# GpSimd's elementwise work in the norms and in the MLP is given to VectorE and ScalarE

## The chip, the core and the metric

The kernel runs on one core of one Trainium2 chip. A core has a matrix engine (TensorE), two elementwise engines (VectorE and ScalarE), a third, programmable one (GpSimd, POOL in the profile) and SyncE, which here issues the DMAs. Each engine works through its own list of instructions in order; semaphores connect the lists. The metric is the device time of one execution in microseconds, the median of several runs.

## The reference, cut to what matters

Two layers work on a sequence of 1024 frames of width 1024, in float32. Each layer is

```python
mixed = hybrid_mixer(rmsnorm(h, norm_pre_mix[l]), ...)   # mLSTM, GLA and retention heads
h = h + rmsnorm(mixed, norm_post_mix[l])
ff = square(relu(rmsnorm(h, norm_pre_ffn[l]) @ w_ff1[l])) @ w_ff2[l]     # d_ff = 4096
h = h + rmsnorm(ff, norm_post_ffn[l])
# rmsnorm(x, g) = x * rsqrt(mean(x * x, axis=-1) + 1e-6) * g
```

The four rmsnorms of a layer and the square between the two MLP products are what the change is about. The mixer's GLA part, with its chunks of scores built in seven levels, stays as it is.

## The kernel before, in words

Activations are kept transposed: a tile holds 128 features (partitions) by 512 frames, and eight such tiles are one half of the sequence. Each layer is done half by half.

Every large product has float32 accuracy out of three passes: both operands are split into a high part (rounded to float32r) and a low part (the rest), and `mm3` (lines 267 to 270) issues low x high, high x low, high x high. `wslot` (253) loads a 512-row block of weights, casts it on ScalarE (263) and subtracts on VectorE (264); three such blocks may be alive. `split` (272) does the same with an activation: cast on ScalarE (276), subtraction (277). `fm_group` (280) computes two 128x512 output tiles in the two PSUM buffers tagged `d`; a buffer can be refilled only after its evacuation `evac` has read it.

The MLP of one half (`ffn_steps`, 861) runs in eight chunks of 512 hidden features. `f1` is the first product: each of its 128x512 results is read out of PSUM by a Relu on ScalarE (873), squared into the high part on ScalarE (876), squared once more at full precision on GpSimd (877), and the low part is the difference on VectorE (878). `f2` is the second product, whose results are added to an accumulator on VectorE (897). `f1` of a chunk is issued two chunks ahead of the `f2` that reads it. There are 4 x 32 results of `f1`.

A norm has a sum of squares over the eight tiles, a matmul with a matrix of ones that adds over the partitions and hands the sum to every partition (`rstd_begin`, 331), a reciprocal square root on ScalarE and VectorE (`rstd_end`, 336), and the scaling:

- `out_proj` (838) evacuates each of its eight tiles on ScalarE (846), squares it on ScalarE (857) and adds it to `sso` (858), with a lower priority; the add is on GpSimd, but for the last, which is on VectorE.
- `post_norm_end` (383) has two VectorE instructions for each tile, 390 and 391, the second of which adds the residual.
- `square_sum` (345) squares the resulting eight tiles on ScalarE (350, 353) and adds seven of them (354): four on GpSimd, the last three on VectorE. The squares share three buffers of the tag `nt` with the tiles of `pre_norm_end`.
- `pre_norm_end` (362) scales each tile on VectorE (366) and splits it: cast on ScalarE, subtraction on VectorE, but for tiles 2 and 5 on GpSimd.

`mix_norms` (1012) chains a post-norm, the sum and a pre-norm after a mixer, `ffn_norms` (1030) the same after an MLP. These and the mixers are generators: the main list of products calls `tick` after each output tile, and the generator goes on by a step, so that small matmuls are put between large ones. TensorE's order is thereby written out; where a generator's matmul waits, all later products wait behind it.

On the other engines the order is set by a planner when the program is built: it takes the instructions that are ready by its own account of costs, highest priority first. Evacuations have 9000, weight blocks 6000, the norms 2500, the sums of `out_proj` 1500. On the chip the order is fixed, and an instruction at the head of an engine's list that has to wait holds up all behind it.

The main program begins at line 1126. Norms run beside products in four places: `mix_norms(0, 0)` at about 385 to 435 us, `ffn_norms(0, 0)` and `mix_norms(0, 1)` at about 850 to 1000 us, the same pair one half later (1450 to 1600 us), and `mix_norms(1, 1)` at about 2035 to 2095 us.

Of the kernel before, what the change touches and what calls it, by code (L numbers as in the profile page):

```python
# [10 lines left out]
F32 = mybir.dt.float32  # L11
# [3 lines left out]
AF = mybir.ActivationFunctionType  # L15
ALU = mybir.AluOpType
# [3 lines left out]
P = 128  # L20
# [3 lines left out]
KT = D // P  # L24
NH = 2
TH = T // NH
# [20 lines left out]
def hybrid_trunk(ctx, tc, a, out):  # L47
    nc = tc.nc
    V, S, G = nc.vector, nc.scalar, nc.gpsimd
# [23 lines left out]
    tp = ctx.enter_context(tc.tile_pool(name="tp", bufs=4))  # L73
# [67 lines left out]
    def pcol(l, key, i):  # L141
        if key == "mixn":
            c = 64 + 4 * l + i if i < 4 else 72 + 2 * l + i - 4 if i < 6 else 76 + 2 * l + i - 6
        elif key == "conv":
            c = 80 + 16 * l + i
        elif key == "gbias":
            c = 112 + l
        else:
            c = {"pre_mix": 0, "post_mix": 16, "pre_ffn": 32, "post_ffn": 48}[key] + 8 * l + i
        return prm[:, c:c + 1]  # L150
# [121 lines left out]
    def split(src, name, eng=V):  # L272

        hi = up.tile([P, TH], F32R, tag="uh", name=f"uh_{name}")
        lo = up.tile([P, TH], F32R, tag="ul", name=f"ul_{name}")
        S.copy(out=hi, in_=src)  # L276
        eng.tensor_tensor(out=lo, in0=src, in1=hi.bitcast(F32), op=ALU.subtract)  # L277
        return hi, lo

    def fm_group(w, u, evac, name):  # L280

        nk = w.shape[0] // 512
        sl = [wslot(w[512 * k:512 * (k + 1), :], 256, f"{name}_{k}") for k in range(nk)]
        ps = [pd.tile([P, 512], F32, tag="d", name=f"d_{name}_{m}") for m in range(2)]
        for k in range(nk):
            for m in range(2):
                for j in range(4):
                    uh, ul = u[4 * k + j]
                    mm3(ps[m], sl[k][0][:, j, m * P:(m + 1) * P], sl[k][1][:, j, m * P:(m + 1) * P],
                        uh, ul, k == 0 and j == 0, k == nk - 1 and j == 3)  # L290
                if k == nk - 1:
                    with tc.high_priority(offset=EPRIO):
                        rest = evac(m, ps[m])
                    if rest:
                        with tc.high_priority(offset=RPRIO):
                            rest()
                tick()
# [47 lines left out]
    def square_sum(tiles, name):  # L345
        ss = None
        for kt in range(KT):
            if kt == 0:
                ss = np_.tile([P, TH], F32, tag="ss", name=f"ss_{name}", bufs=3)
                S.activation(out=ss, in_=tiles[0], func=AF.Square)  # L350
            else:
                sq = np_.tile([P, TH], F32, tag="nt", name=f"sq_{name}_{kt}", bufs=3)
                S.activation(out=sq, in_=tiles[kt], func=AF.Square)
                (V if kt >= KT - 3 else G).tensor_tensor(out=ss, in0=ss, in1=sq, op=ALU.add)
        return ss

    def pre_norm(h, l, key, name):

        ss = square_sum(h, name)
        return pre_norm_end(h, rstd_of(ss, name), l, key, name)  # L360

    def pre_norm_end(h, r, l, key, name):
        u = []
        for kt in range(KT):
            w = np_.tile([P, TH], F32, tag="nt", name=f"w_{name}_{kt}", bufs=3)
            V.scalar_tensor_tensor(out=w, in0=h[kt], scalar=pcol(l, key, kt), in1=r, op0=ALU.mult, op1=ALU.mult)
            u.append(split(w, f"{name}_{kt}", G if kt in (2, 5) else V))
        return u

    def post_norm(half, acc, ss, l, key, name, store):  # L370
# [467 lines left out]
    def out_proj(pj, y, tiles=None):  # L838
        l, n = pj.l, pj.n
        acc = []  # L840
        ss = np_.tile([P, TH], F32, tag="ss", name=f"sso{n}", bufs=3)
        for g in range(4):
            def ev(m, ps):
                kt = 2 * g + m
                t = tiles[kt] if tiles else accp.tile([P, TH], F32, tag="acc", name=f"o{n}_{kt}")
                S.copy(out=t, in_=ps)
                acc.append(t)
                return lambda: block_sq(ss, t, tp.tile([P, TH], F32, tag="tmp", name=f"bo{n}_{kt}"), kt, G if kt < KT - 1 else V)
            fm_group(a["w_out"][l][:, 256 * g:256 * (g + 1)], y, ev, f"out{n}_{g}")
        return acc, ss  # L850

    def block_sq(ss, src, sq, kt, eng=V):

        if kt == 0:
            S.activation(out=ss, in_=src, func=AF.Square)
        else:
            S.activation(out=sq, in_=src, func=AF.Square)
            eng.tensor_tensor(out=ss, in0=ss, in1=sq, op=ALU.add)


    def ffn_steps(l, half, u, late=False, done=None):

        n = f"{l}{half}"
        st = {"acc": [None] * KT, "ss": None}
        hid = {}
        NCH = DFF // 512

        def f1(c, g):
            def ev(m, ps):
                f = 2 * g + m  # L870
                nm = f"hid{n}_{c}_{f}"
                r = tp.tile([P, TH], F32, tag="tmp", name=f"r_{nm}")
                S.activation(out=r, in_=ps, func=AF.Relu)  # L873
                hi = up.tile([P, TH], F32R, tag="uh", name=f"h_{nm}")
                lo = up.tile([P, TH], F32R, tag="ul", name=f"l_{nm}")
                S.activation(out=hi, in_=r, func=AF.Square)  # L876
                G.tensor_tensor(out=r, in0=r, in1=r, op=ALU.mult)  # L877
                V.tensor_tensor(out=lo, in0=r, in1=hi.bitcast(F32), op=ALU.subtract)  # L878
                hid[(c, f)] = (hi, lo)
            col = 512 * c + 256 * g  # L880
            fm_group(a["w_ff1"][l][:, col:col + 256], u, ev, f"f1{n}_{c}_{g}")

        def scratch(kt):
            if not late:
                return np_.tile([P, TH], F32, tag="nt", name=f"bf{n}_{kt}", bufs=3)
            return tp.tile([P, TH], F32, tag="tmp", name=f"bf{n}_{kt}")

        def f2(c, g):
            def ev(m, ps):
                kt = 2 * g + m  # L890
                if c == 0:
                    t = accp.tile([P, TH], F32, tag="acc", name=f"f{n}_{kt}")
                    V.tensor_copy(out=t, in_=ps)
                    st["acc"][kt] = t
                else:
                    t = st["acc"][kt]
                    V.tensor_tensor(out=t, in0=t, in1=ps, op=ALU.add)  # L897
                if c == NCH - 1:
                    if kt == 0:
                        st["ss"] = np_.tile([P, TH], F32, tag="ss", name=f"ssf{n}", bufs=3)  # L900
                    def rest():
                        sq = scratch(kt)
                        if done and kt == KT - 1:
                            S.activation(out=sq, in_=t, func=AF.Square)
                            st["last"] = sq
                        else:
                            block_sq(st["ss"], t, sq, kt)
                        if done:
                            done(kt, t)
                    return rest  # L910
            fm_group(a["w_ff2"][l][512 * c:512 * (c + 1), 256 * g:256 * (g + 1)], [hid[(c, f)] for f in range(4)], ev, f"f2{n}_{c}_{g}")

        steps = [lambda c=c, g=g: f1(c, g) for c in range(2) for g in range(2)]
        for c in range(NCH):
            steps += [lambda c=c, g=g: f2(c, g) for g in range(4)]
            if c + 2 < NCH:
                steps += [lambda c=c, g=g: f1(c + 2, g) for g in range(2)]
        return steps, st
# [90 lines left out]
    u0, rn0, rows0, _ = x_in(0, sl0)  # L1009
    ffn = {}  # L1010

    def mix_norms(l, half, acc, ss, res, gap):

        hl = residual(half, f"pm{l}{half}")
        for _ in range(gap[0]):
            yield 1
        n = f"pm{l}{half}"
        ps = rstd_begin(ss, n)
        with tc.high_priority(offset=NPRIO):
            h = post_norm_end(half, acc, rstd_end(ps, ss, n), l, "post_mix", n, True, hl)  # L1020
            n = f"uf{l}{half}"
            ss = square_sum(h, n)
        for _ in range(gap[1]):
            yield 1
        ps = rstd_begin(ss, n)
        with tc.high_priority(offset=NPRIO):
            res["u"] = pre_norm_end(h, rstd_end(ps, ss, n), l, "pre_ffn", n)
        res["h"] = h
# [124 lines left out]
    r = {}  # L1153
# [102 lines left out]
```

## Time and profile before

| | |
|---|---|
| median of 3 runs | 2483.89 us (2482.72 to 2485.12) |
| the profiled execution | 2483.34 us |
| its span, first to last instruction | 2481.6 us |
| TensorE busy | 2413.4 us, 97% |
| VectorE busy | 1572.0 us, 63% |
| ScalarE busy | 1065.6 us, 43% |
| GpSimd busy | 299.7 us, 12%, in 253 instructions |
| mean granted clock of TensorE | 0.995 of full speed |

A time in the rows is the latency of an instruction. Two VectorE instructions that follow each other overlap, so the second begins before the first has ended. In the answers an idle time before an instruction stands in brackets with what ended it. Rows of a timeline begin with the start in us from the span's start, and the duration in us.

### The profile page before, as it was taken

How to read it: one execution, taken by the hardware profiler on the slowest of the kernel's cores; microseconds unless marked ns; L12 is line 12 of the kernel's file. 1: busy time of each engine (PE TensorE's matmuls, PEld its weight loads, DVE VectorE, ACT ScalarE, POOL GpSimd, SP SyncE). 2: the span in 40 equal slices, each digit the busy share in tenths (PEclk: the TensorE clock that was granted, in tenths of full speed). 3: DMA queues.
4: the chain of work that ended last, by engine and by line, in shares of the span. 5: the costliest groups of instructions: out<-in, count | busy, mean ns of one | idle time of the engine just before them, and what ended most of it. 6: DMA issues, size and time to landing. Idle time of an engine off the chain costs nothing. (4 is left out here: it accounts for less than half of the span.)

```text
span 2481.6 us, 31329 instructions
## 1 busy us (share of the span) xinstructions
PE 2413.4 (97%) x11436; PEld 1981.8 (80%) x11436; DVE 1572.0 (63%) x2800; ACT 1065.6 (43%) x2050; POOL 299.7 (12%) x253
## 2 busy tenths in 40 slices
PE   8999998999999989999999999999999999999998
PEld 7778887788788778888788878888888887888886
DVE  5888757756755685856755576776865538634434
ACT  6666344433333454633423344553433344423233
POOL 0000011101111120010110022010110012111010
PEclk9999999999999999999999999999999999999999
DMA  8645454333334355523423445543323433433331
GB/s 252 204 132 170 143 174 153 105 95 116 103 104 151 125 170 172 151 91 108 127 78 117 157 144 165 178 129 109 117 87 93 138 126 111 145 94 94 94 95 67
DMA packets 324246, 321.61 MB, mean 130 GB/s; under 512 B 15434, under 2 KB 292476, under 8 KB 324092
## 3 DMA queue, kind: packets, MB, share of 16 engines
q1 hardware_dynamic: 324092, 319.61, 41.7%
q8 instruction: 90, 1.47, 0.3%
q14 instruction: 64, 0.52, 0.1%
HBM read 263.92 MB, written 55.64 MB: 129 GB/s over the span
## 5 line engine op out<-in xcount | busy, mean ns | idle before, releaser
L263 ACT CAST h_f<-r_f 128x1024 fp32r<-128x1024 f32 x256 | 267.7, 1046 | 558.1 <-PE d_f L270 553.1
L264 DVE TENSOR_TENSOR l_f<-r_f,h_f 128x1024 fp32r<-128x1024 f32 x256 | 319.3, 1247 | 181.3 <-ACT h_f L263 178.3
L268 PE MATMUL d_f<-h_hid,l_f 128*128 128x512 f32 x1024 | 417.9, 408 | 8.6 <-DVE f L897 7.1
L268 PE MATMUL d_f<-uh_uf,l_f 128*128 128x512 f32 x1024 | 417.0, 407 | 4.3 <-ACT uh_uf L276 4.3
L269 PE MATMUL d_f<-ul_uf,h_f 128*128 128x512 f32 x1024 | 406.5, 397 | 0.1
L269 PE MATMUL d_f<-l_hid,h_f 128*128 128x512 f32 x1024 | 406.4, 397 | 0.0
L270 PE MATMUL d_f<-uh_uf,h_f 128*128 128x512 f32 x1024 | 403.3, 394 | 0.0
L270 PE MATMUL d_f<-h_hid,h_f 128*128 128x512 f32 x1024 | 402.9, 393 | 0.0
L877 POOL TENSOR_TENSOR r_hid<-r_hid 128x512 f32<-128x512 f32 x128 | 163.9, 1280 | 1127.5 <-ACT h_hid L876 1127.5
L897 DVE TENSOR_TENSOR f<-f,d_f 128x512 f32<-128x512 f32 x224 | 153.4, 685 | 140.1 <-PE d_f L270 139.6
L268 PEld LDWEIGHTS d_f<-h_hid,l_f 128*128 128x128 f32 x1024 | 193.6, 189 | 58.6 <-DVE f L897 9.4
L268 PEld LDWEIGHTS d_f<-uh_uf,l_f 128*128 128x128 f32 x1024 | 193.7, 189 | 49.7 <-ACT uh_uf L276 4.5
L270 PEld LDWEIGHTS d_f<-uh_uf,h_f 128*128 128x128 f32 x1024 | 192.8, 188 | 44.4
L270 PEld LDWEIGHTS d_f<-h_hid,h_f 128*128 128x128 f32 x1024 | 192.7, 188 | 43.9
L269 PEld LDWEIGHTS d_f<-ul_uf,h_f 128*128 128x128 f32 x1024 | 193.1, 189 | 42.2 <-issue 1.2
L269 PEld LDWEIGHTS d_f<-l_hid,h_f 128*128 128x128 f32 x1024 | 192.9, 188 | 42.5 <-issue 2.4
L878 DVE TENSOR_TENSOR l_hid<-r_hid,h_hid 128x512 fp32r<-128x512 f32 x128 | 89.4, 698 | 163.4 <-POOL r_hid L877 162.5
L264 DVE TENSOR_TENSOR l_in<-r_in,h_in 128x1024 fp32r<-128x1024 f32 (+2 forms) x96 | 122.0, 1271 | 74.4 <-ACT h_in L263 74.3
L873 ACT ACTIVATE r_hid<-d_f 128x512 f32<-128x512 f32 x128 | 76.5, 598 | 195.4 <-PE d_f L270 195.3
L263 ACT CAST h_in<-r_in 128x1024 fp32r<-128x1024 f32 (+2 forms) x96 | 101.4, 1056 | 47.7 <-PE d_in L270 39.2
L269 PE MATMUL d_in<-ul_u,h_in 128*128 128x512 f32 x256 | 101.9, 398 | 4.6 <-DVE ul_u L277 4.6
L268 PE MATMUL d_in<-uh_x,l_in 128*128 128x512 f32 x256 | 104.9, 410 | 1.1 <-DVE px L446 0.9
(394 smaller groups left out, 4261.3 us busy)
## 6 DMA issues: line engine op xcount, KB each, us to landing
r_f<-in_w_ff_dram SPq DMA_DIRECT2D x256, 512.0 KB, 3.7
r_in<-in_w_in_dram SPq DMA_DIRECT2D x80, 512.0 KB, 4.0
r_out<-in_w_out_dram SPq DMA_DIRECT2D x32, 512.0 KB, 3.5
pv<-pv SPq DMA_DIRECT2D x64, 128.0 KB, 2.4
pf<-px SPq DMA_DIRECT2D x32, 256.0 KB, 4.2
vt<-pv SPq DMA_DIRECT2D x32, 256.0 KB, 3.9
pg<-gz_g SPq DMA_DIRECT2D x32, 256.0 KB, 2.0
gt<-pg SPq DMA_DIRECT2D x32, 256.0 KB, 4.6
```

Source lines behind the costliest of these rows:

```text
L263: S.copy(out=hi[:, :, :n], in_=raw[:, :, :n])
L264: V.tensor_tensor(out=lo[:, :, :n], in0=raw[:, :, :n], in1=hi[:, :, :n].bitcast(F32), op=ALU.subtract)
L268: nc.tensor.matmul(ps, al, bh, start=start, stop=False)
L269: nc.tensor.matmul(ps, ah, bl, start=False, stop=False)
L270: dense[0] = nc.tensor.matmul(ps, ah, bh, start=False, stop=stop)
L873: S.activation(out=r, in_=ps, func=AF.Relu)
L877: G.tensor_tensor(out=r, in0=r, in1=r, op=ALU.mult)
L878: V.tensor_tensor(out=lo, in0=r, in1=hi.bitcast(F32), op=ALU.subtract)
L897: V.tensor_tensor(out=t, in0=t, in1=ps, op=ALU.add)
```

## The change

The sums of squares of `square_sum` and of `out_proj` are all added on VectorE, and all the subtractions of `split` are on VectorE. In `f1`, the square is computed once, at full precision, on ScalarE, and cast to the high part by a second ScalarE instruction. GpSimd keeps the memsets and line 619, the diagonal of the GLA scores.

```diff
@@ square_sum
-                (V if kt >= KT - 3 else G).tensor_tensor(out=ss, in0=ss, in1=sq, op=ALU.add)
+                V.tensor_tensor(out=ss, in0=ss, in1=sq, op=ALU.add)
@@ pre_norm_end
-            u.append(split(w, f"{name}_{kt}", G if kt in (2, 5) else V))
+            u.append(split(w, f"{name}_{kt}"))
@@ out_proj
-                return lambda: block_sq(ss, t, tp.tile(...), kt, G if kt < KT - 1 else V)
+                return lambda: block_sq(ss, t, tp.tile(...), kt)
@@ ffn_steps, f1
-                S.activation(out=hi, in_=r, func=AF.Square)
-                G.tensor_tensor(out=r, in0=r, in1=r, op=ALU.mult)
+                S.activation(out=r, in_=r, func=AF.Square)
+                S.copy(out=hi, in_=r)
                 V.tensor_tensor(out=lo, in0=r, in1=hi.bitcast(F32), op=ALU.subtract)
```

`split` and `block_sq` take VectorE where no engine is given. The number of DMAs, matmuls and tiles is unchanged.

## Rows read from the trace of the kernel before

**Rows 1.** The page's first part: busy time, share, instructions of three engines.
```profile
PE 2413.4 (97%) x11436; PEld 1981.8 (80%) x11436; DVE 1572.0 (63%) x2800; ACT 1065.6 (43%) x2050; POOL 299.7 (12%) x253
```

**Rows 2.** Busy time in windows: two norm stretches; sum of four MLP stretches.
```profile
391.00:412.00 21.00, 17.50 (x105) 15.01 (x103) 20.73 (x25) 7.72 (x12) 6.30 (x5) 0.99 0.69 240
...
2042.00:2060.00 18.00, 12.34 (x53) 9.37 (x51) 18.00 (x19) 7.07 (x11) 9.63 (x6) 1.00 0.39 133
...
sum 1430.00, PE 1426.87 PEld 1161.26 DVE 806.51 ACT 500.62 POOL 161.02; mean PE 356.72 PEld 290.32 DVE 201.63 ACT 125.16 POOL 40.26
```

**Rows 3.** Waits of PE, 385 to 470 us: total, times, longest.
```profile
PE d_f L268 <- ACT uh_uf L276: 4.3, 1, 4.3
PE nps_uf L62 <- DVE ss_uf L354: 2.8, 1, 2.8
...
PE d_in L268 <- ACT sq_uf L353: 0.4, 1, 0.4
```

**Rows 4.** Waits of PE, 850 to 960 us.
```profile
PE d_in L269 <- DVE ul_u L277: 2.3, 2, 1.6
PE d_in L268 <- ACT gst L460: 2.2, 1, 2.2
PE d_out L268 <- ACT o_Pg L846: 1.5, 1, 1.5
...
PE d_out L268 <- ACT o_cv L846: 0.3, 1, 0.3
```

**Rows 5.** Waits of PE, 2030 to 2100 us.
```profile
PE d_f L268 <- DVE f L897: 5.3, 1, 5.3
PE d_f L268 <- ACT r_hid L873: 0.5, 1, 0.5
```

**Rows 6.** Timeline of DVE in a post-norm: start, duration.
```profile
392.89 1.41 DVE L391 SCALAR_TENSOR_TENSOR o<-o,prm,hl_pm_k 128x512 f32<-128x512 f32 x2
394.22 1.28 DVE L390 TENSOR_TENSOR o<-o,sso 128x512 f32<-128x512 f32 x2
395.42 1.79 DVE L391 SCALAR_TENSOR_TENSOR o<-o,prm,hl_pm_k 128x512 f32<-128x512 f32 x1
...
922.57 1.78 DVE L391 SCALAR_TENSOR_TENSOR o_Pg<-o_Pg,prm,hl_pm_E 128x512 f32<-128x512 f32 x1
```

**Rows 7.** Timeline of POOL beside it.
```profile
395.04 1.62 POOL L354 TENSOR_TENSOR ss_uf<-ss_uf,sq_uf 128x512 f32<-128x512 f32 x1 [17.39 <-ACT sq_uf L353]
```

**Rows 8.** Groups of POOL and DVE: busy, mean ns, idle before them.
```profile
L877 POOL TENSOR_TENSOR r_hid<-r_hid 128x512 f32<-128x512 f32 x128 | 163.9, 1280 | 1127.5 <-ACT h_hid L876 1127.5
L858 POOL TENSOR_TENSOR sso<-sso,bo 128x512 f32<-128x512 f32 x24 | 38.5, 1604 | 244.9 <-ACT bo L857 244.9
...
L391 DVE SCALAR_TENSOR_TENSOR o_rqk<-o_rqk,prm,hl_pm_vt 128x512 f32<-128x512 f32 x3 | 2.2, 739 | 0.0
```

**Rows 9.** Windows after three waits of PE; the third number from the right is its clock.
```profile
412.00:415.00 3.00, 3.00 (x9) 1.97 (x10) 0.27 (x1) 0.96 (x2) 0.00 (x0) 0.52 0.94 261
1528.00:1537.00 9.00, 6.79 (x42) 6.58 (x42) 5.56 (x7) 4.42 (x12) 0.11 (x1) 0.81 0.85 250
2060.00:2066.00 6.00, 5.88 (x19) 4.74 (x20) 5.64 (x9) 2.73 (x4) 0.00 (x0) 0.72 0.65 203
```

**Rows 10.** Timeline of ACT in an MLP with nothing beside it.
```profile
2273.72 0.60 ACT L873 ACTIVATE r_hid<-d_f 128x512 f32<-128x512 f32 x1 [1.79 <-PE d_f L270]
2274.36 0.63 ACT L876 ACTIVATE h_hid<-r_hid 128x512 fp32r<-128x512 f32 x1
...
2277.00 1.04 ACT L263 CAST h_f<-r_f 128x1024 fp32r<-128x1024 f32 x1
...
2284.84 0.60 ACT L873 ACTIVATE r_hid<-d_f 128x512 f32<-128x512 f32 x1 [1.79 <-PE d_f L270]
```

**Rows 11.** Group of ACT: a cast of a 128x512 tile.
```profile
L276 ACT CAST uh_uf<-w_uf 128x512 fp32r<-128x512 f32 x32 | 19.6, 620 | 23.5 <-DVE w_uf L366 23.0
```

**Rows 12.** Waits of DVE: sums that stand on DVE already.
```profile
DVE ssf L858 <- ACT bf L857: 9.2, 12, 1.2
```

More of the change, by code (lines that the diff above doesn't have):

```diff
@@ L847, in ev @@
                 acc.append(t)
-                return lambda: block_sq(ss, t, tp.tile([P, TH], F32, tag="tmp", name=f"bo{n}_{kt}"), kt, G if kt < KT - 1 else V)
+                return lambda: block_sq(ss, t, tp.tile([P, TH], F32, tag="tmp", name=f"bo{n}_{kt}"), kt)
             fm_group(a["w_out"][l][:, 256 * g:256 * (g + 1)], y, ev, f"out{n}_{g}")
```

## The prediction

> **What bounds the kernel now.** I read the busy shares first. TensorE is busy 97% of the span, VectorE 63%, ScalarE 43%, GpSimd 12% [rows 1]. So time can be won only where TensorE idles or runs slowly, at most 68 us. Second, the busy time by stretch, to find those places. Four MLP stretches, 1430 us together, hold 1426.87 us of matmul: nothing done there is worth more than 3.1 us. In the norm stretches VectorE is full: 20.73 of 21 us, and 18.00 of 18 us, where TensorE has 12.34 [rows 2]. Third, TensorE's waits there. I call the places A (385 to 435 us), B (850 to 960), C (one half later, 1450 to 1560: its waits repeat B's to 0.1 us) and D (2030 to 2095).
>
> A: 4.3 us for the cast of the first scaled tile, 2.8 for the sum of squares, and two waits of 0.4 [rows 3]. B, and C again: 2.3 for low parts of scaled tiles, 2.2 and 1.5 + 0.3 for evacuations on ScalarE [rows 4]. D: 5.3 for an evacuation on VectorE and 0.5 for one on ScalarE [rows 5]. Together 7.9 + 2 x 6.3 + 5.8 = 26.3 us.
>
> Fourth, the timeline, for why VectorE is late. Line 391 takes 739 ns unhindered [rows 8], 1.79 us where a GpSimd add began 0.4 us before it [rows 6, 7]: 1.05 us more, and again 1.04 (1.78) as the last such case of B [rows 6]. I call this a hit. There is one for each GpSimd instruction while VectorE is full: four in A, seven, three and four in the three stretches of B (before the waits of 1.5, 2.3 and 2.2 us), as many in C, six in D (two of them from squares of the MLP). That is 38. ScalarE's late evacuations have the same cause: they stand behind squares that wait for line 391.
>
> Last, the clock. After the waits TensorE runs for some microseconds at the lower of its two levels (1.2 instead of 2.4 GHz): the granted clock was 0.52 over 3 us in A, 0.81 over 9 in C, 0.72 over 6 in D [rows 9], which cost 0.48 x 3 = 1.4, 0.19 x 9 = 1.7 and 0.28 x 6 = 1.7 us.
>
> **The change part by part.**
>
> *Sums and subtractions, GpSimd to VectorE.* Two instructions in a row take 1.28 us where one takes about 0.68, so one more costs the queue 0.60 us [rows 6]. Where VectorE is full, each exchange takes away a hit of 1.04 and adds 0.60: 0.44 us won, although VectorE gets more work.
>
> - A: four adds, 1.8 us off the wait of 2.8. The two waits of 0.4 are for instructions behind hits, and go: 0.8. The 4.3 stay: from the sum to the first scaled tile nothing changes, and the products that fill that time are the same. Of the 1.4 us of slow clock I take half, 0.7. Sum 3.3.
> - B: seven exchanges before the 1.5 + 0.3 are worth 3.1, so both go: 1.8. Three before the 2.3 (one add of line 858, two subtractions): 1.3. Four before the 2.2: 1.8. Sum 4.9.
> - C: 4.9, and half of 1.7 us of clock: 5.8.
> - D: six hits go (6.2), four adds come (2.4): 3.8 off the 5.3. The 0.5 goes. Half of the 1.7 us of clock is 0.8. Sum 5.1.
>
> Together 19.1 us. What is late next: in A the scaled tiles (4.3), in D what is left of the evacuation, 1.5.
>
> Most of the 24 adds of line 858 [rows 8] stand beside products while VectorE isn't full and are hidden by that; the matmul that reads their sum stands four products further on. Without that cover each costs 0.60.
>
> An add now waits on VectorE for its square on ScalarE. Behind it stand the next tiles' lines 390 and 391, weight subtractions, and evacuations, on which TensorE waits. Bounds of that wait: nothing, where the planner puts the add after other work, or 0.77 us as in the twelve sums of the MLP that wait on VectorE already (9.2 / 12, [rows 12]). I take nothing: those twelve were put on an idle VectorE, these have eight tiles of other work to stand behind.
>
> *The square of the MLP, GpSimd to ScalarE.* 128 squares of 1.28 us [rows 8] leave GpSimd, and their hits VectorE; 128 casts of 0.62 us [rows 11] come to ScalarE, 79 us. Alone with an MLP, ScalarE has for two results 2 x (0.60 + 0.63) and two weight casts of 1.04, 4.5 us of the 11.12 from one pair to the next [rows 10]; with the casts 5.8. The evacuation (873) comes first in each triple, so only the next result's can be late. The high and low parts are read two chunks later, so their own delay, which even shrinks, counts for nothing. The cover is thin only beside mixers, whose ScalarE instructions come in bursts. Bounds: 3.1 us gained (the idle time of the MLP stretches, [rows 2]), or two casts of 0.62 late in each of the twelve mixer chunks and six convolutions beside MLPs, 18 x 1.24 = 22.3 us lost. I take 2 lost, near the first, since [rows 2] shows TensorE hardly ever waiting there.
>
> *Order.* No DMA and no matmul moves in the program's text, but the planner orders VectorE's and ScalarE's lists anew. Its order before was made for a VectorE that the hits then delayed; without them the chip should follow it better. I price that at zero and leave it in the range.
>
> Sum: 19.1 - 2 = 17.1 us off the profiled execution's 2483.34 (a span of 2481.6 and 1.7 around it), 2466.2. The median of the runs is 0.55 above that execution, so 2467.
>
> The Trainium skill speaks against this change: the page "Perfetto Trace Analysis", section "Optimizing Scalar/DVE Operations", says that where VectorE is saturated it may pay to hand work to ScalarE or even to GpSimd. VectorE is saturated here, and by that rule alone the 36 instructions that come to it in A to D would add 36 x 0.60 = 21.6 us, 2505. The same passage warns that the two share a read port, and the rows side with the warning.
>
> The skill's page "SBUF — State Buffer", section "Who interferes with whom", states that a VectorE instruction with two SBUF inputs and a GpSimd instruction that reads SBUF shut each other out for a whole instruction. By it a hit is what is left of the GpSimd instruction, 1.62 - 0.38 = 1.24 us in the pair shown, and the 38 would weigh 7 us more; the trace has 1.05.
>
> **The rivals.**
>
> 1. *Everything goes.* If VectorE keeps pace, no wait is left in A to D, none of the 4.8 us of slow clock, and the MLP's 3.1 us go too: 34.2 us, 2450. For it: all these waits trace back to hits. Against it: the chain after the sum in A has none until its tiles are being scaled.
> 2. *ScalarE's waits stay.* Evacuations on ScalarE are held up by squares in front of them, and these still follow a VectorE list that got longer. Then only A (1.8 and 0.7), the low parts in B and C (1.3 each) and D (3.8 and 0.8) win: 9.7 - 2 = 7.7, 2476. For it: the waits of 2.2 and 1.5 name ScalarE. Against it: line 391, for which the squares wait, comes earlier.
> 3. *The casts meet the bursts.* The 22.3 us above in full against the 19.1: 2487, no change. For it: ScalarE can't reorder. Against it: 3.1 us in 1430.
> 4. *Slower: the adds wait at the head of VectorE's list.* With 0.77 us each, the 36 moved instructions take 36 x 1.37 = 49.3 us of a full VectorE and free 38 x 1.04 = 39.5: 9.8 us more, 2494. It decides from a wait of 39.5 / 36 - 0.60 = 0.50 us on. For it: the twelve sums that wait so today. Against it: they wait where there is nothing else to do.
>
> That the change doesn't do what it says can't be: all four edits are plain changes of engine.
>
> **How the numbers follow.** Forecast 0.55; rival 1 0.08, rival 2 0.17, rival 3 0.09, rival 4 0.11. The forecast's own range is 2462 to 2474 (the clock in full or not at all is 2.4 us to each side, the casts 0 to 6). From 2455 to 2488 leaves out rival 1 and rival 4, 2 in 10. No change is 0.2% to either side, 2479 to 2489, about what a measurement of this kernel can tell. Faster has the forecast, rivals 1 and 2, less 0.04 of these for an unlucky new order: 0.76; the same has rival 3 and that 0.04: 0.13; slower 0.11.
>
> **What would show it.** GpSimd's busy time falls by more than the 202 us of lines 877 and 858 [rows 8]. Line 391 is at 0.74 us in all its groups. The wait for the sum in A is near 1.0, the evacuation in D below 2, the ScalarE waits of B and C gone, the 4.3 in A still there. MLP stretches stay within some 2 us of full. The prediction is wrong if sums on VectorE wait over 0.5 us each for their squares, if matmuls of the MLP wait for line 873, or if idle time turns up in stretches that now have none.

## The result and the profile after

The changed kernel takes 2444.89 us, the median of 3 runs (2442.43 to 2449.56), against 2483.89: a ratio of 0.9846, interval 0.9821 to 0.9870. That is 39.0 us faster. The direction is the one forecast; the forecast was 17 us, and its range ended at 2455. Beside the experiments the same kernel took 2443.91 (2439.69 to 2445.70, 4 runs) against 2482.84: 0.9843, interval 0.9830 to 0.9857. So the miss is no accident of three runs. Only rival 1 ("everything goes", 2450, held at 0.08) comes near.

The first part of the page, changed kernel ([rows 1] before):

```profile
PE 2405.4 (98%) x11436; PEld 1983.0 (81%) x11436; DVE 1545.7 (63%) x2860; ACT 1142.3 (47%) x2178; POOL 30.0 (1%) x65
```

VectorE has 60 instructions more and is busy 26.3 us less. At the 0.60 to 0.68 us that such an instruction adds, the 60 are 36 to 41 us of work, so by this estimate 62 to 67 us of the 1572.0 before were not work: they were VectorE instructions being held up.

The waits of TensorE from 385 to 470 us, changed kernel (total, times, longest; [rows 3] before):

```profile
PE d_f L268 <- ACT uh_uf L276: 7.7, 1, 7.7
PE st L65 <- DVE st L533: 0.5, 1, 0.5
PE nps_uf L62 <- DVE ss_uf L354: 0.3, 1, 0.3
```

From 850 to 960 us, and again from 1450 to 1560, this one row is all that answers to [rows 4], and from 2000 to 2100 us ([rows 5]) there is none:

```profile
PE d_in L269 <- DVE l_in L264: 0.2, 1, 0.2
```

B, C and D have no stop left. A has kept one, which grew from 4.3 to 7.7 us. VectorE's timeline in D of the changed kernel (start, duration) has no hit, and shows where the planner put the adds of line 354, namely behind the evacuations of line 897 ([rows 6] before):

```profile
2028.14 0.69 DVE L897 TENSOR_TENSOR f<-f,d_f 128x512 f32<-128x512 f32 x1
2028.74 0.75 DVE L391 SCALAR_TENSOR_TENSOR o_rqk<-o_rqk,prm,hl_pm_vt 128x512 f32<-128x512 f32 x1
...
2030.92 0.69 DVE L897 TENSOR_TENSOR f<-f,d_f 128x512 f32<-128x512 f32 x1 [0.29 <-PE d_f L270]
2031.52 2.14 DVE L354 TENSOR_TENSOR ss_uf<-ss_uf,sq_uf 128x512 f32<-128x512 f32 x3
```

**Where the 39 us come from.** Busy time by stage shows it best (width, then busy time of PE, PEld, DVE, ACT and POOL; the third number from the right is TensorE's clock). First the kernel before, then the changed kernel, as profiled beside the experiments (span 2443.0 us):

```profile
0.00:385.00 385.00, 361.34 (x1960) 305.71 (x1961) 272.78 (x639) 223.85 (x520) 21.45 (x43) 1.00 0.58 176
385.00:435.00 50.00, 42.17 (x204) 34.05 (x203) 43.85 (x57) 23.40 (x38) 9.54 (x7) 0.90 0.51 169
435.00:850.00 415.00, 411.52 (x1849) 333.36 (x1848) 264.63 (x519) 152.84 (x313) 47.88 (x43) 1.00 0.37 112
850.00:960.00 110.00, 103.22 (x571) 87.84 (x570) 86.30 (x94) 56.34 (x101) 34.26 (x21) 1.00 0.55 168
960.00:1450.00 490.00, 488.31 (x2233) 399.09 (x2232) 305.09 (x579) 200.77 (x385) 46.25 (x38) 1.00 0.39 121
1450.00:1560.00 110.00, 103.65 (x566) 88.37 (x565) 83.16 (x91) 58.24 (x103) 31.78 (x19) 0.98 0.54 166
1560.00:2000.00 440.00, 437.42 (x2011) 357.26 (x2010) 279.17 (x545) 182.62 (x363) 43.35 (x35) 1.00 0.39 121
2000.00:2095.00 95.00, 89.22 (x374) 71.12 (x373) 61.92 (x75) 41.99 (x61) 24.07 (x15) 0.98 0.38 122
```

```profile
0.00:385.00 385.00, 365.65 (x1967) 310.03 (x1968) 276.36 (x646) 224.44 (x521) 11.95 (x37) 0.99 0.58 176
385.00:435.00 50.00, 41.14 (x215) 34.37 (x214) 41.64 (x63) 25.82 (x42) 0.10 (x1) 0.93 0.55 177
435.00:850.00 415.00, 414.49 (x1868) 337.29 (x1867) 266.80 (x529) 174.42 (x348) 6.55 (x11) 1.00 0.37 113
850.00:960.00 110.00, 109.77 (x610) 94.69 (x609) 85.94 (x126) 61.88 (x107) 0.32 (x3) 1.00 0.60 187
960.00:1450.00 490.00, 490.00 (x2237) 400.64 (x2237) 303.51 (x576) 221.09 (x422) 4.97 (x6) 1.00 0.40 122
1450.00:1560.00 110.00, 109.77 (x640) 96.04 (x640) 80.40 (x117) 59.49 (x103) 0.21 (x2) 1.00 0.60 188
1560.00:2000.00 440.00, 439.75 (x1992) 358.60 (x1991) 266.49 (x526) 198.20 (x390) 5.88 (x5) 1.00 0.38 118
2000.00:2095.00 95.00, 95.00 (x424) 76.25 (x423) 79.17 (x111) 52.83 (x81) 0.00 (x0) 1.00 0.39 124
```

Width less PE is TensorE's idle time. Over the whole span it falls from 2481.6 - 2413.4 = 68.2 to 2443.0 - 2403.6 = 39.4 us, by 28.8. The other 9.8 us of the 38.6 are time in which TensorE counts as busy: matmuls at the lower clock, or drawn out behind a stop. Set against the forecast, by the start of the same matmul in these two traces:

| stretch | forecast, us won | measured |
|---|---|---|
| ahead of A | 0 | 1.9 |
| A | 3.3 | 2.1 |
| MLP, A to B | | 4.3 |
| B | 4.9 | 8.0 |
| B to C | | 2.3 |
| C | 5.8 | 8.7 |
| C to D | | 3.3 |
| D | 5.1 | 7.8 |
| MLPs, all three | -2 | 9.9 |
| sum | 17.1 | 38.4 |

The row "ahead of A" is no gain: in the first profile of the same kernel (span 2447.8 us) it is -3.0, while every other row agrees with this one within 0.2 us.

VectorE's durations say the same: between 385 and 435, 840 and 960, 1440 and 1560, and 2020 and 2095 us, the durations before lie 45.5 us above the median of the same line and shape in the changed kernel, and 45 instructions lie over 0.25 us above it; in the changed kernel none does. The 38 hits of the forecast were 39.5 us.

### The profile page after: what moved, and what is told of

It is laid out like the page before. It is cut to its first block, busy times and chain, and to the rows that moved or that the text cites. A ratio compares the mean times of both kernels' runs of the same rounds, so it can differ in the third digit from the quotient of the medians.

```text
span 2447.8 us, 31038 instructions
## 1 busy us (share of the span) xinstructions
PE 2405.4 (98%) x11436; PEld 1983.0 (81%) x11436; DVE 1545.7 (63%) x2860; ACT 1142.3 (47%) x2178; POOL 30.0 (1%) x65
## 4 chain that ended last, share of the span: by engine, by line
PE 86%; DVE 3%; DMA 1%; ACT 1%; issue 1%; SPq 0%; DVEq 0%; ACTq 0%
PE d_f L269 19%; PE d_f L268 19%; PE d_f L270 19%; PE d_in L269 5%; PE d_in L268 5%; PE d_in L270 4%; PE d_out L268 2%; PE d_out L269 2%; PE d_out L270 2%; PE gr L62 2%; PE gs L62 1%; PE mn L62 1%; PE ms L62 1%; PE yp L65 1%; PE mu L62 1%
## 5 line engine op out<-in xcount | busy, mean ns | idle before, releaser
L264 DVE TENSOR_TENSOR l_f<-r_f,h_f 128x1024 fp32r<-128x1024 f32 x256 | 313.3, 1224 | 205.9 <-ACT h_f L263 202.4
L263 ACT CAST h_in<-r_in 128x1024 fp32r<-128x1024 f32 (+2 forms) x96 | 101.4, 1056 | 49.6 <-PE d_in L270 39.4
L268 PE MATMUL d_in<-uh_u,l_in 128*128 128x512 f32 x256 | 102.6, 402 | 0.0
L269 PE MATMUL d_in<-ul_x,h_in 128*128 128x512 f32 x256 | 102.1, 399 | 0.0
```

Of the source, the lines that this page charges most:

```text
L263: S.copy(out=hi[:, :, :n], in_=raw[:, :, :n])
L264: V.tensor_tensor(out=lo[:, :, :n], in0=raw[:, :, :n], in1=hi[:, :, :n].bitcast(F32), op=ALU.subtract)
L268: nc.tensor.matmul(ps, al, bh, start=start, stop=False)
L269: nc.tensor.matmul(ps, ah, bl, start=False, stop=False)
```

## The experiments

Each is set against runs of the kernel before on the same chip: 2482.84 us beside the repeat, the kernel without sums and those with GpSimd's reads or writes put back; 2482.74 beside the three parts and the sums twice; 2484.2 beside the rest.

**The changed kernel again.** Its times stand above.

> The changed kernel again, on the chip of the three that follow. 2445 us, within 5: its three runs so far went from 2442 to 2450.

**The parts one by one**, each put into the kernel before. First the sums alone:

```diff
-                (V if kt >= KT - 3 else G).tensor_tensor(out=ss, in0=ss, in1=sq, op=ALU.add)
+                V.tensor_tensor(out=ss, in0=ss, in1=sq, op=ALU.add)
-                return lambda: block_sq(..., kt, G if kt < KT - 1 else V)
+                return lambda: block_sq(..., kt)
```

> The first part of the change alone: the 48 sums on VectorE; the square of the MLP and two subtractions of each pre-norm stay on GpSimd. My recorded sum, 0.44 an exchange: A 3.3, B 4.0, C 4.9, D 2.3, 14 us: 2470. 'Hits in full' (the planner puts the additions behind what TensorE waits for, so that each hit counts 1.04): 20 to 25 us, 2459 to 2464, as with the sums left out.

Measured: 2459.53 us, ratio 0.9913 (0.9898 to 0.9927), 23.2 us won.

The square of the MLP alone:

```diff
-                S.activation(out=hi, in_=r, func=AF.Square)
-                G.tensor_tensor(out=r, in0=r, in1=r, op=ALU.mult)
+                S.activation(out=r, in_=r, func=AF.Square)
+                S.copy(out=hi, in_=r)
```

> The second part alone: the square of the MLP's first product on ScalarE, its cast too. Recorded: two hits of D gone (2.1), 2 lost to the casts: 2484. 'Hits in full': 2.1 in D with a stop less, and the small waits of the MLP stretches for lines 893, 897 and 533, some 4 us: 2476 to 2480. The rival that the casts meet ScalarE's bursts: up to 2506.

Measured: 2474.58 us, 0.9965 (0.9953 to 0.9978), 8.2 us won. The evacuation on which D waits 5.3 us before [rows 5] is waited for 2.1 us here (waits of TensorE, 2000 to 2110 us):

```profile
PE d_f L268 <- DVE f L897: 2.1, 1, 2.1
```

That is not the two hits alone. VectorE's timeline in D of the kernel before has what the forecast overlooked:

```profile
2036.26 0.69 DVE L878 TENSOR_TENSOR l_hid<-r_hid,h_hid 128x512 fp32r<-128x512 f32 x1 [2.95 <-POOL r_hid L877]
...
2041.89 0.69 DVE L878 TENSOR_TENSOR l_hid<-r_hid,h_hid 128x512 fp32r<-128x512 f32 x1 [0.93 <-POOL r_hid L877]
```

Twice VectorE stands still at the head of its list, 3.9 us in all, for a square that GpSimd hasn't finished, and the whole post-norm waits behind it. Over the program that comes to this (waits of VectorE, kernel before):

```profile
DVE l_hid L878 <- POOL r_hid L877: 162.5, 102, 3.8
```

The subtractions of the pre-norm alone (`split(w, ...)` without GpSimd):

> The third part alone: all subtractions of the pre-norms on VectorE. Recorded: two exchanges in B and in C before the wait for low parts, 1.8 us: 2482. 'Hits in full': two hits of 1.04 in each, up to the 2.3 us waited there and a stop: 4 to 5 us, 2479.

Measured: 2476.18 us, 0.9978 (0.9970 to 0.9987, 11 runs from 2472.61 to 2481.67), 6.6 us won. The three parts make 23.2 + 8.2 + 6.6 = 38.0 us, the whole 38.9. In the total, and within the noise of these runs, the parts neither share a gain nor depend on each other.

**The sums left out**, in the kernel before, VectorE's list as it was:

```diff
-                (V if kt >= KT - 3 else G).tensor_tensor(out=ss, in0=ss, in1=sq, op=ALU.add)
+                if kt >= KT - 3: V.tensor_tensor(out=ss, in0=ss, in1=sq, op=ALU.add)
-            eng.tensor_tensor(out=ss, in0=ss, in1=sq, op=ALU.add)
+            if eng: eng.tensor_tensor(out=ss, in0=ss, in1=sq, op=ALU.add)
```

> The kernel before with the 48 sums of GpSimd left out (each sum of squares lacks these tiles); VectorE's list is that of before. 'Hits': 32 of 38 hits go and VectorE gets nothing to do: 20 to 25 us off, 2459 to 2464. 'Order': 2480 to 2484, since the list is the old one. My recorded sum (an addition on VectorE takes back 0.60 of every 1.04) lets this kernel be up to 32 x 0.60 = 19 us better than the one with these sums moved to VectorE; if the additions cost nothing, the two are equal.

Measured: 2459.68 us, 0.9909 (0.9895 to 0.9922), 23.2 us won. Adding the sums on VectorE also won 23.2: doing 48 adds there costs nothing that can be seen against not doing them at all. The new order of the lists isn't the reason either, since this kernel has the old one. The page shows the hold-ups directly:

```profile
PE 2411.2 (98%) x11436; PEld 1982.4 (81%) x11436; DVE 1534.1 (62%) x2800; ACT 1065.6 (43%) x2050; POOL 215.4 (9%) x205
```

The same 2800 instructions of VectorE are busy 37.9 us less than before [rows 1]. In the kernel that adds the sums on VectorE it is busy 1564.2 us: 30.1 us of work more, in the same time.

**The sums twice**, in the changed kernel: each of the 48 moved adds is issued a second time.

> The changed kernel with each of the 48 moved sums issued twice in a row on VectorE (each of these squares counts double). Recorded: a sum costs the path 0.60 us wherever VectorE is full, 30 of the 48 do: up to 18 us more, 2463. 'Hits in full' says that the sums lie behind what TensorE waits for: 2445 to 2450, with A alone paying, 4 x 0.60 = 2.4.

Measured: 2457.09 us, 0.9897 (0.9884 to 0.9911), 13.2 us slower than the changed kernel. So the room on VectorE is not endless. Waits of TensorE over the whole program:

```profile
PE nps_uf L62 <- DVE ss_uf L354: 5.6, 1, 5.6
PE d_in L268 <- ACT uh_u L276: 5.3, 2, 2.7
PE d_f L268 <- ACT uh_uf L276: 5.1, 1, 5.1
```

The first and the last stand in A, the 2.7 each in B and C (880 to 890 us and one half later); D still has none. 48 adds more are 48 x 0.60 = 28.8 us of VectorE, of which 13.2 are paid. In A that isn't VectorE's room alone: no product is left there between the sum and the scaled tiles (ten in the changed kernel).

**The sums early** in VectorE's list. This tests, on the adds of line 354 (those of line 858 stay where they are), the explanation that I had by then: that the moved adds are free because the planner put them behind what TensorE waits for.

```diff
-                V.tensor_tensor(out=ss, in0=ss, in1=sq, op=ALU.add)
+                with tc.high_priority(offset=4000): V.tensor_tensor(out=ss, in0=ss, in1=sq, op=ALU.add)
```

> The changed kernel with the additions of the norms' sums of squares (line 354) put early in VectorE's list, between lines 390 and 391, by a higher priority; in the changed kernel they stand behind the last line 391 and behind the evacuations. Same instructions, same number. Theory 'the moved sums were free because of where they stand': early, each costs its 0.60 us, and a wait for its square on top. D has an evacuation of line 897 behind some four of them (2.4 us, of which 0.9 us were slack in the kernel before: 1.5), B and C each four ahead of the last tile (2.4 less 2.0 of slack) and three before the scaled tiles (1.8 less 0.8): 0.4 + 1.0 each, so 1.5 + 2.8 = 4.3 us and 0.3 for each of five stops, 1.5: 2446 to 2452, more where they wait for squares. Rival 'VectorE has room for one more instruction per tile wherever it stands': 2442 to 2446, no wait of TensorE in B, C and D.

Measured: 2440.54 us, 0.9830 (0.9816 to 0.9844), not to be told from the changed kernel's 0.9843. My explanation fell. The rival's sign, no wait in B, C and D, held; the time is 1.5 us below its range. VectorE's timeline in D shows that the adds did go to the front, and there is no wait of TensorE from 2000 to 2100 us, nor in B or C:

```profile
2019.12 0.68 DVE L354 TENSOR_TENSOR ss_uf<-ss_uf,sq_uf 128x512 f32<-128x512 f32 x1
2019.72 0.74 DVE L391 SCALAR_TENSOR_TENSOR o_Pg<-o_Pg,prm,hl_pm_E 128x512 f32<-128x512 f32 x1
...
2021.52 0.68 DVE L897 TENSOR_TENSOR f<-f,d_f 128x512 f32<-128x512 f32 x1
```

**Reads of GpSimd put back**, without any work taken from another engine: in the changed kernel GpSimd adds each of the 48 squares to itself, into a tile that nobody reads.

```diff
+    ghost = lambda sq: G.tensor_tensor(out=tp.tile([P, TH], F32, tag="hl", name="ghost", bufs=2), in0=sq, in1=sq, op=ALU.add)
+                if kt < KT - 3: ghost(sq)
+            if shadow: ghost(sq)
```

> The changed kernel, with VectorE's, ScalarE's and TensorE's lists as they are, and 48 GpSimd additions put beside the 48 moved sums: each reads the same square and writes a tile that nobody reads. Theory 'hits' (the gain is the hits that go): 32 of the 38 hits of A to D are back, 1.04 us each, and most of the waits with them, some 20 us: 2460 to 2472. Rival 'order' (the gain is the planner's new lists, which are kept here): 2445, as the changed kernel.

Measured: 2467.90 us, 0.9941 (0.9929 to 0.9954): 24.0 us of the gain are gone. In the traces the lists of VectorE, ScalarE and TensorE are those of the changed kernel, instruction for instruction, so rival 'order' is out.

**The same with writes alone**, two memsets of the tile for each add:

```diff
+    def ghost(act):
+        t = tp.tile([P, TH], F32, tag="hl", name="ghost", bufs=2)
+        for _ in range(2): after(G.memset(t, 0.0), act)
```

> As the one before, but GpSimd fills the tile with zeros twice (2 x 0.53 us) in the place of each addition, released by the same squares: as busy, but it reads nothing from SBUF. If the hits come from GpSimd's reads: 2445, and line 391 stays at 0.74 us. If any GpSimd work, or its writes, hold VectorE up: 2460 to 2472, as with the additions.

Measured: 2443.67 us, 0.9845 (0.9832 to 0.9858): nothing lost. VectorE's timeline in B, first the kernel with reads, then, two lines further down in its file, the one with memsets:

```profile
852.47 1.41 DVE L391 SCALAR_TENSOR_TENSOR f<-f,prm,hl_pf_k 128x512 f32<-128x512 f32 x2
...
856.14 2.98 DVE L391 SCALAR_TENSOR_TENSOR f<-f,prm,hl_pf_E 128x512 f32<-128x512 f32 x2
```

```profile
847.10 1.41 DVE L393 SCALAR_TENSOR_TENSOR f<-f,prm,hl_pf_k 128x512 f32<-128x512 f32 x2
...
850.76 1.41 DVE L393 SCALAR_TENSOR_TENSOR f<-f,prm,hl_pf_E 128x512 f32<-128x512 f32 x2
```

and what GpSimd did beside them, in the same order:

```profile
853.97 6.05 POOL L226 TENSOR_TENSOR ghost<-sq_u 128x512 f32<-128x512 f32 x3 [70.29 <-ACT sq_u L353]
```

```profile
850.03 1.11 POOL L228 MEMSET ghost<- 128x512 f32 x2 [0.36 <-ACT sq_u L355]
```

A pair of lines takes 2.98 us beside reads and 1.41 beside memsets, and VectorE's whole list is busy 1574.4 us beside reads, 1544.5 beside memsets and 1544.9 in the changed kernel. The Trainium skill's page "SBUF — State Buffer", section "Who interferes with whom", says that a VectorE instruction with two SBUF inputs collides with a GpSimd instruction that reads SBUF, "not with one that only writes it". These two runs bear that out.

The 24.0 us, though, aren't all VectorE's lateness. An add also keeps the buffer of its square until GpSimd is done with it; a memset doesn't. In B, and again in C, one add took 5.38 us (the shortest of the 48 took 1.22), the next square on ScalarE waited for its buffer, and TensorE waited for the sum, as it does there neither in the kernel before nor in the changed one (waits of ScalarE, GpSimd's row, waits of TensorE):

```profile
ACT sq_u L353 <- POOL ghost L226: 5.3, 2, 2.7
866.36 5.38 POOL L226 TENSOR_TENSOR ghost<-sq_u 128x512 f32<-128x512 f32 x1 [1.31 <-ACT sq_u L353]
PE nps_u L62 <- DVE ss_u L355: 5.0, 2, 2.5
```

No run puts reads back without holding a buffer, so what each costs TensorE is open.

**Filling the wait in A.** In the changed kernel TensorE has only some 2 us of products, ten matmuls, between the sum and the scaled tiles. One product of the next half is held back until then:

```diff
-    m[1] = 1.75
+    m[1] = 2.0
-    run(main[:4])
+    run(main[:3])
-    run(main[4:5])
+    run(main[3:4])
-    run(main[5:])
+    run(main[4:])
```

> The changed kernel with one more product of the second half's input projection kept back until behind the first output projection (three products stand ahead of it now, not four; the rate at which the mixer is dealt out beside them goes from 1.75 to 2.0 so that it still ends in time). It touches A alone. In the changed kernel TensorE waits 7.7 to 8.5 us there for the cast of the first scaled tile, with 2.1 us of products between the sum and the wait. Theory 'the wait in A is an empty place, which any 8 us of products fill': the 8.5 us go, and with them the slow clock behind them (10 us at half the clock in the profiled executions, about 5 us): 8 to 13 us off 2443.9, so 2431 to 2436. Rival 'VectorE or the mixer is what ends last in A': the products come later, but the mixer ahead of the output projection now ends later by as much, and the time stays within 3 us of 2443.9.

Measured: 2434.34 us (2431.91 to 2435.04), 0.9800 (0.9787 to 0.9813), clear of the changed kernel's interval and some 10 us below it: the fastest kernel here. The wait of 8.5 us is gone, and with it the slow clock; the window of A has 1.00 for the clock where it had 0.93 (waits of TensorE from 380 to 450 us, then the window):

```profile
PE nps_uf L62 <- DVE ss_uf L354: 0.9, 1, 0.9
PE st L65 <- DVE st L533: 0.4, 1, 0.4
PE d_f L269 <- DVE ul_uf L277: 0.4, 1, 0.4
PE d_f L268 <- ACT r_hid L873: 0.2, 1, 0.2
```

```profile
385.00:435.00 50.00, 48.03 (x250) 39.20 (x249) 41.69 (x67) 27.50 (x46) 0.45 (x3) 1.00 0.57 181
```

**GpSimd's last reads moved too**, on top of that: line 619, eight instructions, to VectorE.

```diff
-        G.tensor_tensor(out=Pg8, ..., op=ALU.mult)
+        V.tensor_tensor(out=Pg8, ..., op=ALU.mult)
```

> As the kernel with one more product behind the output projection (2431 to 2436 by the first theory), and the last of GpSimd's instructions that read SBUF, the diagonal of line 619 (8 instructions of 1.9 to 2.3 us), moved to VectorE too. Theory 'every GpSimd read beside a busy VectorE holds it up, but only where TensorE waits for VectorE does it count': TensorE has no wait near these eight, so the time is the other kernel's within 2 us. Rival 'reads count wherever they stand': up to 8 x (2.3 - 0.7) = 13 us less.

Measured: 2437.76 us, 0.9817 (0.9803 to 0.9832), 3.4 us above the kernel without it, though the two intervals overlap. There is no gain, so the rival is out: these eight reads cost nothing where they stand, although VectorE is busy 4.1 us less without them (1541.1 for 1545.2) with eight instructions more. The first theory's 2 us are missed by a little, on the slow side.

## Why the prediction was wrong

**What held.** The mechanism, that VectorE instructions are held up while GpSimd reads SBUF, and that A to D wait for VectorE because of it: the 48 adds taken off GpSimd take 37.9 us off VectorE's busy time and win 23.2, and reads put back lengthen it again by 29.5 us where writes don't. ScalarE's waits in B and C went, as forecast against rival 2. The adds don't wait for their squares in A to D; only five of line 858 do, beside products (8.8 us in all, and TensorE waits for none of them). So rival 4 was out. Line 391 is at 0.74 to 0.75 us everywhere. GpSimd's busy time fell by 269.7 us, more than 202.

**The step that failed in B, C and D: "one more costs the queue 0.60 us"**, and with it the 0.44 us for an exchange. B, C and D won 24.5 us where the forecast had 15.8. It took VectorE for full because [rows 2] has it busy for 20.73 of 21 us and 18.00 of 18. But an instruction that is held up counts as busy for as long as it is held. In the whole of B (850 to 960 us) 16.7 of VectorE's 86.3 busy us are durations above the changed kernel's medians, in C 15.6 of 83.2. Take them off and there is room, which the moved adds use: with and without them the time is the same (23.2 us won either way), and even at the front of the list those of line 354 make TensorE wait nowhere in B, C or D. As far as these two points show, the price is a step, not a slope: the first 48 adds cost nothing that can be seen, the next 48 cost 13.2 us. With the full 1.04 us for each hit the forecast's own waits of B, C and D would have gone entirely: 6.3 + 6.3 + 5.8 = 18.4 us, where it counted 4.9 + 4.9 + 4.3 = 14.1 without the clock. That is still less than the 24.5 measured there; the rest is what follows.

**D: a wait of VectorE for GpSimd.** The forecast looked for hits and priced the square's two, at 1.04 us each; in the trace those two are 0.78 (1.52 us for 0.74). It didn't ask what VectorE itself waits for: 3.9 us at the head of the list for line 877, ahead of the whole post-norm. With the square alone moved, the wait for line 897 fell by 3.2 us.

**The casts: the wrong sign, and the largest term of the miss.** The MLP stretches won 9.9 us where the forecast had -2. With the square alone, 8.2 us were won in all; in its trace 7.0 lie in these stretches and 5.0 in D, less some 2 elsewhere. The bound of 3.1 us came from four windows chosen inside the MLPs; the stretches between A, B, C and D as a whole had 3.5 + 1.7 + 2.6 = 7.8 us of idle TensorE, and 0.8 are left. Between A and B, TensorE's waits before were for VectorE (lines 533, 897 and 893: 1.5, 1.0 and 0.8 us); with the square alone moved, 0.5 us is left. Whether VectorE was late there from hits or from standing for line 877, no run separates. ScalarE took the 128 casts without a wait of TensorE for line 873 over 0.25 us.

**The clock and the stops, too small.** I took half of the slow clock in A, C and D. In C and D all of it went: the clock is 1.00 in both stages, from 0.98. And a stop costs more than its idle time. In the kernel before, the first matmul behind a wait is drawn out even at full clock (the first row; the clock is 1.00 there, [rows 2]), and behind D's long wait the same kind of matmul takes up to twice as long, there at the lower clock [rows 9]:

```profile
2051.81 0.50 PE L268 MATMUL d_f<-h_hid,l_f 128*128 128x512 f32 x1 [0.52 <-ACT r_hid L873]
...
2054.47 0.39 PE L270 MATMUL d_f<-h_hid,h_f 128*128 128x512 f32 x1
2060.12 0.79 PE L268 MATMUL d_f<-h_hid,l_f 128*128 128x512 f32 x1 [5.26 <-DVE f L897]
2060.71 0.63 PE L269 MATMUL d_f<-l_hid,h_f 128*128 128x512 f32 x1
```

The forecast left out that drawn-out first matmul. With each matmul's busy time set against that of the same matmul in the changed kernel, 3.6 of the 9.8 us by which TensorE's busy time fell lie in stretches at the lower clock, 5.7 at 40 matmuls behind a wait in one trace or the other (mostly 0.50 us where the same one adds 0.23 without the wait), and 0.5 elsewhere. The profile models the ends of matmuls, so this is an estimate.

**A: "the 4.3 stay" was wrong the other way.** The forecast took it that the products which fill that time are the same. They aren't, for TensorE's list changed too. The sum's matmul and the first product of the scaled tiles, in the kernel before and in the changed one:

```profile
411.89 2.08 PE L62 MATMUL nps_uf<-ss_uf,ones 128*128 128x512 f32 x2 [2.75 <-DVE ss_uf L354]
...
422.59 1.22 PE L268 MATMUL d_f<-uh_uf,l_f 128*128 128x512 f32 x2 [4.27 <-ACT uh_uf L276]
```

```profile
408.93 1.12 PE L62 MATMUL nps_uf<-ss_uf,ones 128*128 128x512 f32 x2 [0.28 <-DVE ss_uf L354]
...
419.75 1.22 PE L268 MATMUL d_f<-uh_uf,l_f 128*128 128x512 f32 x2 [8.52 <-ACT uh_uf L276]
```

From the one to the other it is 10.7 us before and 10.8 after (10.0 in the first profile of the changed kernel): the chain is about as long. But 33 matmuls of the input projection stood between them before, and 10 stand there now; the other 23 come ahead of the sum. So part of what A won ahead of the sum went into that wait, which became 7.7 to 8.5 us. The sums bring this about: with them alone on VectorE 10 matmuls stand there, with them left out 33. So TensorE's order isn't wholly written out by the program's text; moving an add to another engine changed it. One product more in that place, and the wait is gone.

**What stays open.** The sums alone win 23.2 us, but the runs don't split these between line 354 and line 858, nor between VectorE's own lateness and the ScalarE squares that follow it. In A, how much the chain from the sum to the scaled tiles could be shortened was not tried.

## What to carry to other kernels

Before you call an engine full, take off the time by which its instructions run over their own unhindered duration: a held-up engine looks busy, and once the hold-up goes there is room for more work. Then price a removed stall in full, and an added instruction only from the point where that room ends. After the change read again which wait is left and what stands in front of it in TensorE's list, and see whether work that is already there can be put beside it; here moving one product won 10 us more.

## What the runs showed of the hardware that I had not expected

GpSimd's writes didn't hold VectorE up at all: beside 96 memsets of 128x512 its list was busy 1544.5 us and the kernel took 2443.67, beside 48 adds that read 1574.4 and 2467.90. GpSimd is slowed as well: an add that can take 1.22 us took 5.38 beside a VectorE that worked without a pause.

That the 48 reads cost 24.0 us when put back, and moving the real adds won 23.2, is not the same loss undone. By stage, the reads cost 0.6, 9.3, 9.6 and 2.2 us in A, B, C and D, where moving the adds alone had won 2.9, 5.9, 6.6 and 4.8.
